# Projecting the FOX heads 0 to 3 with Strassen chunks that follow the z units

## The chip, the cores and the metric

The kernel runs on one core of a Trainium2 chip. TensorE (PE) multiplies matrices and writes into PSUM; ScalarE (ACT) and VectorE (DVE) work on tiles in SBUF and PSUM; GpSimd (POOL) works on SBUF alone, and it also issues the transfers that add to what they overwrite; SyncE (SP) issues the other transfers between device memory and SBUF. The metric is the time of one launch on the device in microseconds (us), lower is better.

## The reference

One hybrid decoder block over 512 tokens of width 1024, everything float32:

```python
u = rmsnorm(x, norm_mix_g[l])
proj = u @ w_in[l]
(gq, gk, gv, gz, ga, gb, fq, fk, fv, ff, gate_a, gate_b) = jnp.split(proj, split_idx, axis=-1)
...                                   # branch A: conv + SiLU on q, k, v; gated delta rule; norm * silu(z)
o_a = gated_delta_rule_chunked(qh, kh, vh, g, beta).transpose(0, 2, 1, 3)
...                                   # branch B ("FOX"): 8 heads of 128, normalised q and k
o_b = forgetting_attention(fqh, fkh, fvh, log_f).transpose(0, 2, 1, 3)
...
merged = jax.nn.sigmoid(gate_a) * y_a + jax.nn.sigmoid(gate_b) * y_b
h = x + merged @ w_out[l]
x = h + jnp.square(jax.nn.relu(rmsnorm(h, norm_mlp_g[l]) @ w_up[l])) @ w_down[l]
```

The change concerns one part of `proj`: the q, k and v columns of FOX heads 0 to 3, which are 1536 of its columns, `u` (512 x 1024) times a 1024 x 1536 piece of the weights.

## The kernel before

**Numbers.** Every large product is made from float32 operands split in two: `hi` is the operand rounded to the faster matmul type (an ACT cast) and `lo` is the remainder (a DVE subtraction). A product is three matmuls, hi·hi, lo·hi and hi·lo. Weights come as units of 128 x 1024; `seq` lists all units in their order, `unit()` takes the next one, keeps transfers `LA_RAW` = 3 units ahead and the splits `LA_SPLIT` = 2 units ahead.

**Two ways to project.** `dense` (lines 275, 276, 279) makes one block of 128 output columns as 24 matmuls that stream 512 tokens each. `fox_pair` (lines 962, 963, 965) makes the plain product of a panel of 256 columns of FOX heads, with tokens stationary and 256 columns of weights streamed. `stream` (line 1012) makes a chunk of 512 columns by Strassen's scheme (Winograd's form): the 512 x 1024 input and the 1024 x 512 weights are cut in four quarters each, and seven products P1 to P7 of quarters and of sums of quarters take the place of eight. The weights' sums are made by transfers: P1, P2, P3 and P5 are loaded by SP, and P5, P6, P4 and P7 arise when POOL issues a transfer that adds a quarter to the buffer of the product before it (P1, P5, P6, P4 share a buffer, and P3, P7 share one; P5's quarter is added to P1's). The input's sums are made once, by `factors_u`, in the dictionary `uforms`. A product is 24 matmuls of 256 columns. `to` takes the results out of PSUM: ACT copies the first product of a quarter of the output (line 992), DVE adds or subtracts a later one (line 994).

**Order of the work.** The main line is a straight sequence of products. Beside it, generators in `tasks` move on by one step at each `tick()`: the heads of the gated delta rule (`head`), the group's chain (`group_chain`: `invert`, which eliminates on DVE in lines 682 and 684 and multiplies in lines 708 to 742, and then `scan` over four chunks, lines 790 to 819), `decays`, `factors_u` and the `fox_worker`s, each of which takes one FOX head at a time from the list `fq`. A `dense` unit has two ticks, a Strassen product one. `hold[0]` keeps workers from taking a new head. The framework then plans the order on each engine, with the program's order as priority and its own estimate of times, so that what is ready may go ahead of what waits.

The main line before is:

1. The norm and the first z units (`zgate`), `NZ1` = 5 of them, with `normalise` making `uhi` and `ulo`, the split input, and storing the normalised input `xt` to device memory (`ud`).
2. `gdn_group(0)`: 12 projections (heads 0 to 3, three each).
3. `fox_pair(0)`, then `factors_u` is started (it loads `ud` back into tiles named `ux`), then `fox_pair(1)`. Meanwhile group 0's chain runs. One worker is there.
4. `zgate` 5 to 7, then `gdn_group(1)`, 12 projections, under `hold`. The decays of group 1 start when group 0's chain has ended.
5. `stream` over seven chunks: three for FOX heads 4 to 7, four for the two gates. Meanwhile group 1's chain runs, and two workers finish the FOX heads. Near its end `merge_gdn` needs every output of the gated delta rule, through `outputs_in`.
6. The merges, `w_out`, and the MLP, all Strassen products too (line 1172), until the end.

The matrix `AT`, which `head` fills (line 642) and `scan` reads (line 798), has one buffer (`atp`, `bufs=1`) for both groups. Most tiles of 128 x 512 come from one pool of `NPG` = 53 pages.

Of the kernel before, what the change touches and what calls it, by code (L numbers as in the profile page):

```python
# [19 lines left out]
H = 8  # L20
# [19 lines left out]
LA_SPLIT = 2  # L40
INV_STEP = (2500, 900)


def hybrid_block(tc, a, out):
# [65 lines left out]
    def cs(c):  # L110
        return slice(c * P, (c + 1) * P)
# [39 lines left out]
    seq = [("w_ab", 0)] + [("w_z", i) for i in range(NZ1)]  # L151
    seq += [("w_gdn", i) for i in range(12)] + [("w_fox", i) for i in range(12)]
    seq += [("w_z", i) for i in range(NZ1, H)] + [("w_gdn", 12 + i) for i in range(12)]

# [45 lines left out]
    def load(n):  # L200
        nme, i = seq[n]
        if nme in FACTOR:
            w, c, s_ = i
            q, old = FACTOR[nme]
            if old is None:
                if w == "w_st":
                    raw = (swp if nme == "P1" else wraw).tile([P, D], F32, tag="raw", name=nm("sraw"))
                else:
                    raw = fresh[2 if nme == "P2" else s_].tile([P, D], F32, tag="raw", name=nm("draw"))
                nc.sync.dma_start(raw, a[w][c, q, s_])  # L210
            elif (nme, i) in LONE:
                if n not in begun:
                    begin(n)
                raw = begun[n]
                nc.gpsimd.dma_start(raw, a[w][c, 2, s_], accum_op=ALU.add)
            else:
                raw = factors[old, i]
                assert seq.index((old, i)) < len(units)
                nc.gpsimd.dma_start(raw, a[w][c, q, s_], accum_op=ALU.add)
            factors[nme, i] = raw  # L220
            raws[n] = raw, [slice(0, D)]
            return
        w = 256 if nme == "w_ab" else D
        raw = wraw.tile([P, D], F32, tag="raw", name=nm("raw"))
        cuts = [slice(0, 512), slice(512, D)] if 0 < n < 3 else [slice(0, w)]
        for c in cuts:
            nc.sync.dma_start(raw[:, c], a[nme][i][:, c])
        raws[n] = raw, cuts
# [6 lines left out]
    def prefetch_new(n):  # L235

        for m in range(pos[0], min(len(seq), n)):
            if fresh and m not in raws and seq[m][0] in FACTOR and FACTOR[seq[m][0]][1] is None and seq[m][1][0] != "w_st":
                load(m)
            if seq[m] in LONE and m not in begun:  # L240
                begin(m)
# [168 lines left out]
    def normalise():  # L410
        for k in range(KT):
            pool.tensor_tensor(xt[k], xt[k], rb, op=ALU.mult)
            split(xt[k], mix_g[:, k:k + 1], dst=(uh(k), ul(k)))
            nc.sync.dma_start(ud[k], xt[k])
            if k % 2:
                yield


    ud = drp.tile([KT, P, T], F32, tag="ud", name="ud")
    uforms = {}  # L420
# [4 lines left out]
    def factors_u():  # L425
        lo, hi = slice(0, 256), slice(256, 512)
        for part in range(2):
            c = {}
            for k in (2 * part, 2 * part + 1, 2 * part + 4, 2 * part + 5):
                c[k] = page(s="ux")  # L430
                nc.sync.dma_start(c[k], ud[k])
            yield
            yield
# [226 lines left out]
    def invert(AT, rest, ahead):  # L660
# [34 lines left out]
        XT3 = v3(XT[:, :], NI)  # L695

        X2 = sbp.tile([P, NI, 64], F32, tag="sub", name=nm("X2"))
        pool.memset(X2[0:32, :, 32:64], 0.0)
# [140 lines left out]

    def gdn_group(g, box):  # L840
        AT = atp.tile([P, NI, P], F32, tag="AT", name=nm("AT"))
        hd = drp.tile([5, NCH, P, G, P], F32, tag=f"hd{g}", name=f"hd{g}")
        hts = []
        for i in range(G):
            h = g * G + i
            ys = []
            for j in range(3):
                ys.append(project(h, j))
                tick()
            hts.append(start(head(h, AT, *ys, box, hd)))  # L850
        return start(group_chain(g, AT, hd, hts))

# [97 lines left out]

    def fox_pair(hp):
        vts = ([], [])
        for pn in range(3):
            us = [unit("w_fox"), unit("w_fox")]
            pg2 = [page(s="fqk"), page(s="fqk")]
            for t2 in range(2):
                ps = mmps("fx")
                for tb in (2 * t2, 2 * t2 + 1):
                    o = ps[:, (tb % 2) * 256:(tb % 2 + 1) * 256]
                    for k in range(KT):  # L960
                        w = us[k // 4][0][:, (k % 4) * 256:(k % 4 + 1) * 256]
                        mm(o, uhi[k][:, cs(tb)], w, start=(k == 0), stop=False)  # L962
                        mm(o, ulo[k][:, cs(tb)], w, start=False, stop=False)  # L963
                    for k in range(KT):
                        mm(o, uhi[k][:, cs(tb)], us[k // 4][1][:, (k % 4) * 256:(k % 4 + 1) * 256], start=False,  # L965
                           stop=(k == KT - 1))
                    if tb % 2 == 0:
                        tick()
                if pn < 2:
                    act.copy(pg2[t2], ps)  # L970
                else:
                    for j in range(2):
                        (vec.tensor_copy if j else act.copy)(
                            v3(pg2[j][:, 2 * t2 * P:(2 * t2 + 2) * P], 2), v3(ps[:, :], 2)[:, :, cs(j)])
                tick()
            if pn < 2:
                fq.append((2 * hp + pn, pg2, vts[pn]))
            else:
                for v, x in zip(vts, pg2):
                    v += [x[:, cs(c)] for c in range(NCH)]  # L980

    def stream(parts, other):

# [11 lines left out]

        for p, c in STREAM:
            if p is None:
                other()
                continue
# [14 lines left out]
            done = parts[c][2]  # L1014
            at[0] = c
            if p == "P1":
# [73 lines left out]
    start(decays(0, box, gt))  # L1090
    fws = [start(fox_worker())]
    ch0 = gdn_group(0, box)
    fox_pair(0)
    fu = start(factors_u())
    fox_pair(1)
    start(decays(1, box, ch0))
    hold[0] = True
    for h in range(NZ1, H):
        zgate(h)
    ch1 = gdn_group(1, box)  # L1100
    hold[0] = False
    finish(fu)
    fws += [start(fox_worker()) for _ in range(1, NFW)]

# [37 lines left out]
    parts += [gate_chunk(i, to) for to in (sga, mg) for i in range(2)]  # L1142
    stream(parts, merge_gdn)

# [296 lines left out]
def _layout(inputs):  # L1441
# [20 lines left out]
    fx = w[:, 4112:7184].reshape(D, 3, H, P)  # L1462
    pan = []
    for hp in range(2):
        for h in (2 * hp, 2 * hp + 1):
            pan.append(np.concatenate([fx[:, 0, h], fx[:, 1, h]], axis=1))
        pan.append(np.concatenate([fx[:, 2, 2 * hp], fx[:, 2, 2 * hp + 1]], axis=1))
    o["w_fox"] = c(np.stack(pan).reshape(6, 2, 4, P, 256).transpose(0, 1, 3, 2, 4).reshape(12, P, D))
    q, k, v = [[fx[:, j, h] for h in range(H)] for j in range(3)]
# [3 lines left out]

    st = np.stack(st).reshape(7, 2, 4, P, 2, 256)
    o["w_st"] = c(np.stack([st[:, j, :, :, l] for j, l in ((0, 0), (0, 1), (1, 1), (1, 0))], 1)
                  .transpose(0, 1, 3, 2, 4).reshape(7, 4, 1, P, D))
    o["w_z"] = units(w[:, 3072:4096])
# [43 lines left out]
```

## Time and profile before

| what | before |
|---|---|
| median of 3 runs | 977.95 us (977.87 to 978.18) |
| the profiled execution, its own time | 979.09 us |
| its span, first to last instruction | 977.3 us |
| instructions | 17204 |
| PE busy | 968.0 us, 99% of the span |
| DVE, ACT, POOL busy | 709.4, 617.8, 219.5 us |
| granted TensorE clock | 1.000 |
| moved by DMA | 176.50 MB |

The profiled execution took 1.8 us more than its span, and 1.1 us more than the median run. A row of instruction groups gives line, engine, operation, output and inputs, shape and count, then the time that the group kept the engine busy, the mean duration of one in ns, and the idle time ahead of them. A row of the windows gives, for a stretch of the span, the busy time of PE, weight loads, DVE, ACT and POOL with the number of instructions, then the granted clock, the share of DMA and GB/s. A row of the chain gives start, length and what ran. Matmuls overlap, so the duration of one is longer than the spacing between two.

### The profile page before, as it was taken

What the parts mean: (1) busy time and instruction counts of PE and PEld (TensorE: products, weight loads), DVE (VectorE), ACT (ScalarE), POOL (GpSimd) and SP (SyncE); (2) the same over time, 40 slices, a digit from 0 to 9 for tenths busy, and PEclk for the clock granted to TensorE, in tenths of its full rate; (3) what the DMA queues carried; (4) which work ended last, traced back from release to release, by engine and by line L of the source; (5) the groups of instructions that cost most, each with busy time, mean ns of one, the idle gap of its engine ahead of it and who ended that gap; (6) DMA issues with size and microseconds to landing.
All of it is one profiled execution on the core that took longest, in us unless ns stands there. A gap on an engine that the chain in (4) does not pass through costs nothing.

```text
span 977.3 us, 17204 instructions
## 1 busy us (share of the span) xinstructions
PE 968.0 (99%) x6532; PEld 871.9 (89%) x6532; DVE 709.4 (73%) x1206; ACT 617.8 (63%) x1079; POOL 219.5 (22%) x220
## 2 busy tenths in 40 slices
PE   8999999999999999999999999999999999999998
PEld 6788899998888999999998888889989989988986
DVE  6877777656577799855656534889896697698596
ACT  7778654766764787868567412668755765666761
POOL 1503220202313423521320014412121121121110
PEclk9999999999999999999999999999999999999999
DMA  7646872475675987757888726678698888889883
GB/s 267 210 146 191 236 179 88 130 256 175 156 210 163 194 155 169 174 120 175 252 172 234 258 88 191 113 180 173 184 197 192 194 168 203 184 170 205 187 175 110
DMA packets 97634, 176.50 MB, mean 181 GB/s; under 512 B 8160, under 2 KB 53376, under 8 KB 97552
## 3 DMA queue, kind: packets, MB, share of 16 engines
q1 hardware_dynamic: 83088, 122.92, 40.6%
q0 software_dynamic: 14464, 52.49, 30.8%
q8 instruction: 51, 0.84, 0.4%
q14 instruction: 31, 0.25, 0.1%
HBM read 154.34 MB, written 21.04 MB: 179 GB/s over the span
## 4 chain that ended last, share of the span: by engine, by line
PE 91%; ACT 3%; DVE 2%; issue 2%; DMA 1%; POOL 0%; SPq 0%; ACTq 0%; POOLq 0%; DVEq 0%
PE mlp L1172 36%; PE st L1012 13%; PE mm L279 7%; PE mm L276 7%; PE mm L275 7%; PE fx L965 2%; PE fx L962 2%; PE fx L963 2%; PE fo L945 2%; PE sc L920 2%; PE pT L936 1%; ACT hi L256 1%; PE kq L648 1%; PE kk L640 1%; DMA row<-oad 1%
## 5 line engine op out<-in xcount | busy, mean ns | idle before, releaser
L1403 ACT CAST hi<-draw 128x1024 fp32r<-128x1024 f32 x124 | 130.1, 1050 | 118.4 <-PE mlp L1172 101.5
L1410 DVE TENSOR_TENSOR lo<-draw,hi 128x1024 fp32r<-128x1024 f32 x124 | 151.2, 1221 | 44.9 <-ACT hi L1403 42.1
L256 ACT CAST hi<-raw 128x1024 fp32r<-128x1024 f32 (+1 forms) x62 | 62.7, 1020 | 77.6 <-PE mm L276 48.6
L1172 PE MATMUL mlp<-hi,shi 128*128 128x512 f32 x280 | 109.5, 391 | 0.1
L1172 PE MATMUL mlp<-hi,slo 128*128 128x512 f32 x280 | 109.1, 390 | 0.0
L1172 PE MATMUL mlp<-lo,shi 128*128 128x512 f32 x280 | 109.0, 389 | 0.0
L257 DVE TENSOR_TENSOR lo<-raw,hi 128x1024 fp32r<-128x1024 f32 (+1 forms) x62 | 75.4, 1222 | 28.3 <-ACT hi L256 13.6
L1172 PE MATMUL mlp<-slo,hi 128*128 128x256 f32 x448 | 90.3, 283 | 0.0
L1172 PE MATMUL mlp<-shi,lo 128*128 128x256 f32 x448 | 90.3, 283 | 0.0
L1172 PE MATMUL mlp<-shi,hi 128*128 128x256 f32 x448 | 90.3, 283 | 0.0
L276 PE MATMUL mm<-ulo,hi 128*128 128x512 f32 x216 | 84.9, 394 | 1.2 <-DVE ulo L290 1.2
L275 PE MATMUL mm<-uhi,hi 128*128 128x512 f32 x216 | 85.2, 396 | 0.0
L257 DVE TENSOR_TENSOR lo<-sraw,hi 128x1024 fp32r<-128x1024 f32 x49 | 61.6, 1257 | 23.5 <-ACT hi L256 20.1
L1172 PEld LDWEIGHTS mlp<-shi,hi 128*128 128x128 f32 x448 | 70.6, 192 | 0.9
L256 ACT CAST hi<-sraw 128x1024 fp32r<-128x1024 f32 x49 | 51.3, 1047 | 30.7 <-PE st L1012 14.8
L1172 PEld LDWEIGHTS mlp<-shi,lo 128*128 128x128 f32 x448 | 69.9, 192 | 0.0
L1172 PEld LDWEIGHTS mlp<-slo,hi 128*128 128x128 f32 x448 | 69.8, 192 | 0.0
L1172 PEld LDWEIGHTS mlp<-hi,shi 128*128 128x128 f32 x280 | 52.6, 188 | 11.1 <-issue 0.7
L1172 PEld LDWEIGHTS mlp<-lo,shi 128*128 128x128 f32 x280 | 52.6, 188 | 11.1
L1172 PEld LDWEIGHTS mlp<-hi,slo 128*128 128x128 f32 x280 | 52.6, 188 | 10.3
L600 DVE SCALAR_TENSOR_TENSOR conv<-mm,c_conv,conv 128x511 f32<-128x511 f32 (+2 forms) x72 | 53.5, 744 | 5.6 <-ACT conv L597 4.4
L279 PE MATMUL mm<-uhi,lo 128*128 128x512 f32 x216 | 57.1, 402 | 0.0
(337 smaller groups left out, 2389.7 us busy)
## 6 DMA issues: line engine op xcount, KB each, us to landing
draw<-w_u POOLq DMA_DIRECT2D x32, 512.0 KB, 6.0
draw<-w_d POOLq DMA_DIRECT2D x32, 512.0 KB, 6.0
sraw<-w_st POOLq DMA_DIRECT2D x28, 512.0 KB, 6.0
draw<-w_d SPq DMA_DIRECT2D x26, 512.0 KB, 4.3
raw<-w_gdn SPq DMA_DIRECT2D x24, 512.0 KB, 4.3
draw<-w_u SPq DMA_DIRECT2D x24, 512.0 KB, 4.5
sraw<-w_st SPq DMA_DIRECT2D x21, 512.0 KB, 5.2
hd<-hd SPq DMA_DIRECT2D x34, 256.0 KB, 5.5
```

The lines of the kernel that those rows point to most:

```text
L256: act.copy(hi[:, c], raw[:, c])
L257: vec.tensor_tensor(lo[:, c], raw[:, c], hi[:, c].bitcast(F32), op=ALU.subtract)
L275: mm(o, w, rhi(k), start=(k == 0), stop=False)
L276: mm(o, w, rlo(k), start=False, stop=False)
L279: mm(o, lo[:, k * cols:(k + 1) * cols], rhi(k), start=False, stop=(k == KT - 1))
L600: vec.scalar_tensor_tensor(y[:, s:], ps[:, :T - s], cw[:, i:i + 1], y[:, s:], op0=ALU.mult, op1=ALU.add)
L920: mm(psc[:, :n], qT[:, s], kT[:, :n], start=True, stop=True)
L945: mm(po[:, cs(i)], vt[c], st[i][:, cs(c)], start=(c == 0), stop=(c == i))
L1012: mm(o, u, w, start=first and t == 0 and k == 0 and j == 0 and x is hi, stop=x is lo and k == 3, skip_group_check=True)
L1172: return (lambda *args, **kw: tc.keep_in_program_order(f(*args, **kw))) if self.pinned[0] else f
L1403: pact.copy(hi, raws[m][0])
L1410: pvec.tensor_tensor(lo, raws[m][0], hi[:, :].bitcast(F32), op=ALU.subtract)
```

## The change

FOX heads 0 to 3 are projected by `stream` instead of `fox_pair`, as three chunks laid out like those of heads 4 to 7 (new weights `w_sf`; `w_fox` and `fox_pair` go). The list `EARLY` orders their 21 products; near its end, two projections of group 1 and the start of group 1's decays are put between them. The z units 5 to 7 move ahead of the chunks, right behind group 0's projections. `factors_u` is started inside `gdn_group(0)`, after its second head, and works in place on the pages `xt`, which are no longer stored to and loaded from device memory. Both FOX workers exist from the start. Group 0's elimination takes smaller steps between ticks (`INV_STEP`), and `invert` has one more `yield`. Group 1's decays no longer wait for group 0's chain.

```diff
-INV_STEP = (2500, 900)
+INV_STEP = (900, 900)
...
-    seq += [("w_gdn", i) for i in range(12)] + [("w_fox", i) for i in range(12)]
-    seq += [("w_z", i) for i in range(NZ1, H)] + [("w_gdn", 12 + i) for i in range(12)]
+    seq += [("w_gdn", i) for i in range(12)]
+    EARLY = [("P1", 0), ("P2", 0), ("P5", 0), ("P1", 1), ("P3", 0), ("P6", 0), ("P2", 1), ("P7", 0), ("P5", 1), ("P4", 0),
+             ("P3", 1), ("P6", 1), ("P1", 2), ("P2", 2), ("P7", 1), ("P5", 2), ("P4", 1), ("P3", 2), ("P6", 2), (None, 0),
+             ("P7", 2), (None, 1), ("P4", 2), (None, "d")]
+    seq += [("w_z", i) for i in range(NZ1, H)]
+    seq += [(p, ("w_sf", c, 0)) if p else ("w_gdn", 12 + c) for p, c in EARLY if c != "d"]
+    seq += [("w_gdn", 14 + i) for i in range(10)]
...
             split(xt[k], mix_g[:, k:k + 1], dst=(uh(k), ul(k)))
-            nc.sync.dma_start(ud[k], xt[k])
...                                    # in factors_u
             for k in (2 * part, 2 * part + 1, 2 * part + 4, 2 * part + 5):
-                c[k] = page(s="ux")
-                nc.sync.dma_start(c[k], ud[k])
-            yield
+                c[k] = xt[k]
             yield
...                                    # in invert, behind the elimination
+        yield
         X2 = sbp.tile([P, NI, 64], F32, tag="sub", name=nm("X2"))
...
-    def gdn_group(g, box):
+    def gdn_group(g, box, between=None, ahead=()):
...
-                ys.append(project(h, j))
+                ys.append(ahead.pop(0) if ahead else project(h, j))
                 tick()
             hts.append(start(head(h, AT, *ys, box, hd)))
+            if between and i in between:
+                between[i]()
...
-    fws = [start(fox_worker())]
-    ch0 = gdn_group(0, box)
-    fox_pair(0)
-    fu = start(factors_u())
-    fox_pair(1)
-    start(decays(1, box, ch0))
-    hold[0] = True
+    fws = [start(fox_worker()) for _ in range(NFW)]
+    fu = []
+    ch0 = gdn_group(0, box, {1: lambda: fu.append(start(factors_u()))})
     for h in range(NZ1, H):
         zgate(h)
-    ch1 = gdn_group(1, box)
+    finish(*fu)
+    v01, v23 = ([], []), ([], [])
+    ahead = []
+    stream([fox_chunk((None, v01), (0, v01[0])), fox_chunk((2, v23[0]), (1, v01[1])), fox_chunk((3, v23[1]), (None, v23))],
+           EARLY, lambda c: start(decays(1, box)) if c == "d" else ahead.append(project(G, len(ahead))), False)
+    hold[0] = True
+    ch1 = gdn_group(1, box, ahead=ahead)
     hold[0] = False
-    finish(fu)
-    fws += [start(fox_worker()) for _ in range(1, NFW)]
```

More of the change, by code (lines that the diff above doesn't have):

```diff
@@ L205, in load @@
             if old is None:
-                if w == "w_st":
+                if w in ("w_st", "w_sf"):
                     raw = (swp if nme == "P1" else wraw).tile([P, D], F32, tag="raw", name=nm("sraw"))
@@ L237, in prefetch_new @@
         for m in range(pos[0], min(len(seq), n)):
-            if fresh and m not in raws and seq[m][0] in FACTOR and FACTOR[seq[m][0]][1] is None and seq[m][1][0] != "w_st":
+            if fresh and m not in raws and seq[m][0] in FACTOR and FACTOR[seq[m][0]][1] is None and seq[m][1][0] not in ("w_st", "w_sf"):
                 load(m)
@@ L413, in normalise @@
             split(xt[k], mix_g[:, k:k + 1], dst=(uh(k), ul(k)))
-            nc.sync.dma_start(ud[k], xt[k])
             if k % 2:
                 yield
-    ud = drp.tile([KT, P, T], F32, tag="ud", name="ud")
     uforms = {}
@@ L949, in fox_worker, with stream @@
             stores.append(start(store_late(obd[h], o)))
[L951 to L982, printed above, removed]
+    def stream(parts, order, other, main):
         bank = {}
@@ L994, in to @@
                     vec.tensor_tensor(x, x, ps, op=op)
-        for p, c in STREAM:
+        for p, c in order:
             if p is None:
-                other()
+                other(c)
                 continue
@@ L1014, in stream @@
             done = parts[c][2]
-            at[0] = c
+            if main:
+                at[0] = c
             if p == "P1":
@@ L1142, in hybrid_block @@
     parts += [gate_chunk(i, to) for to in (sga, mg) for i in range(2)]
-    stream(parts, merge_gdn)
+    stream(parts, STREAM, lambda c: merge_gdn(), True)
     ot2 = start(outputs_in2())
@@ L1462, in _layout @@
     fx = w[:, 4112:7184].reshape(D, 3, H, P)
[L1463 to L1468, printed above, removed]
     q, k, v = [[fx[:, j, h] for h in range(H)] for j in range(3)]
@@ L1472, in _layout @@
     st += [w[:, n + T * i:n + T * i + T] for n in (7192, 8216) for i in range(2)]
-    st = np.stack(st).reshape(7, 2, 4, P, 2, 256)
-    o["w_st"] = c(np.stack([st[:, j, :, :, l] for j, l in ((0, 0), (0, 1), (1, 1), (1, 0))], 1)
-                  .transpose(0, 1, 3, 2, 4).reshape(7, 4, 1, P, D))
+    sf = [np.concatenate(b, axis=1) for b in
+          ((v[0], v[1], q[0], k[0]), (q[2], k[2], q[1], k[1]), (q[3], k[3], v[2], v[3]))]
+    for name, m in (("w_sf", sf), ("w_st", st)):
+        m = np.stack(m).reshape(len(m), 2, 4, P, 2, 256)
+        o[name] = c(np.stack([m[:, j, :, :, l] for j, l in ((0, 0), (0, 1), (1, 1), (1, 0))], 1)
+                    .transpose(0, 1, 3, 2, 4).reshape(len(m), 4, 1, P, D))
     o["w_z"] = units(w[:, 3072:4096])
```

## The prediction

> **What bounds the kernel now.** I read the page's engine totals first, then the chain, then windows over the stages that the change touches.
>
> ```profile
> span 977.3 us, 17204 instructions
> PE 968.0 (99%) x6532; PEld 871.9 (89%) x6532; DVE 709.4 (73%) x1206; ACT 617.8 (63%) x1079; POOL 219.5 (22%) x220
> ```
>
> PE is busy for 968.0 of 977.3 us, so at most 9.3 us of visible idle time stand against any work taken off it. The windows say where that idle time is not:
>
> ```profile
> 90.00:120.00 30.00, 30.00 (x158) 25.33 (x157) 23.84 (x48) 20.14 (x49) 10.78 (x10) 1.00 0.88 221
> 120.00:137.00 17.00, 17.00 (x141) 16.80 (x140) 10.36 (x22) 9.88 (x29) 2.41 (x3) 1.00 0.78 206
> 137.00:218.00 81.00, 81.00 (x833) 78.46 (x833) 55.61 (x143) 47.14 (x86) 12.94 (x11) 1.00 0.50 156
> 218.00:242.00 24.00, 24.00 (x152) 21.00 (x151) 16.64 (x46) 15.98 (x27) 4.50 (x5) 1.00 0.61 188
> 242.00:320.00 78.00, 77.87 (x396) 65.27 (x395) 53.89 (x94) 47.59 (x110) 21.94 (x21) 1.00 0.64 173
> 320.00:400.00 80.00, 80.00 (x646) 77.28 (x645) 68.36 (x171) 61.19 (x132) 30.74 (x29) 1.00 0.82 176
> 515.00:532.00 17.00, 16.74 (x113) 15.04 (x112) 10.98 (x15) 11.35 (x22) 0.48 (x1) 1.00 0.87 244
> ```
>
> The second number after the length is PE. From 90 to 242 us, which holds the last half of group 0's projections, the plain FOX panels (120 to 218) and the three z units, PE never idles visibly. It also does not idle from 320 to 400, where the existing Strassen chunks of FOX heads 4 to 7 run beside group 1's heads and elimination, although DVE is at 68.36 of 80 us there. So the stage to be replaced is bound by matmul issue, and so is the stage that it will look like. Taking matmuls away should shorten the kernel by their spacing, unless the added work on the other engines makes PE wait.
>
> **What one matmul costs.** Durations overlap, so the price is the spacing, which the chain shows for unbroken runs (start, length, line, count):
>
> ```profile
> 79.32 1.83 PE mm L279 x8
> 123.16 0.96 PE fx L965 x8
> 321.51 2.87 PE st L1012 x24
> 494.14 8.63 PE st L1012 x72
> ```
>
> 0.96/8 = 0.120 us for the plain panels, and 2.87/24 = 0.1196 and 8.63/72 = 0.1199 us for Strassen products. The two kinds cost the same, 0.120 us. The 512-column matmuls of a z unit or a projection cost 1.83/8 = 0.229, so such a unit of 24 takes 5.5 us. The Trainium skill, TensorE: Matmul & The Clock Gate, section "Wait — 56ns, not 53.3ns?", gives N columns divided by 2.4 GHz plus 2.5 ns, 109 ns for 256 columns; the trace's 120 ns disagrees, the trace decides, and by the page the saving below would be 7.9 us.
>
> **The change, part by part.**
>
> *Matmuls removed.* The panels are these:
>
> ```profile
> L962 PE MATMUL fx<-hi,uhi 128*128 128x256 f32 x192 | 48.5, 288 | 0.0
> L963 PE MATMUL fx<-hi,ulo 128*128 128x256 f32 x192 | 47.8, 284 | 0.0
> L965 PE MATMUL fx<-lo,uhi 128*128 128x256 f32 x192 | 28.4, 285 | 0.0
> ```
>
> 3 x 192 = 576 matmuls. After: 3 chunks x 7 products x 24 = 504, of the same 256 columns. 72 fewer, x 0.120 = **8.64 us less** on PE, the path. Everything else on PE (z units, projections, attention, chains) is only moved.
>
> *Work added on ACT, DVE and POOL.* The existing chunks price it:
>
> ```profile
> L256 ACT CAST hi<-sraw 128x1024 fp32r<-128x1024 f32 x49 | 51.3, 1047 | 30.7 <-PE st L1012 14.8 <-DMA sraw<-w_st 7.8 <-PE mm L276 7.1
> L257 DVE TENSOR_TENSOR lo<-sraw,hi 128x1024 fp32r<-128x1024 f32 x49 | 61.6, 1257 | 23.5 <-ACT hi L256 20.1 <-PE mm L279 3.5
> L992 ACT COPY fqk<-st 128x512 f32<-128x512 f32 x12 | 7.0, 584 | 0.0
> L994 DVE TENSOR_TENSOR fqk<-fqk,st 128x512 f32<-128x512 f32 x9 | 6.1, 675 | 2.2 <-ACT fqk L992 2.0 <-ACT hi L256 0.2
> L257 DVE TENSOR_TENSOR lo<-raw,hi 128x1024 fp32r<-128x1024 f32 (+1 forms) x62 | 75.4, 1222 | 28.3 <-ACT hi L256 13.6
> L600 DVE SCALAR_TENSOR_TENSOR conv<-mm,c_conv,conv 128x511 f32<-128x511 f32 (+2 forms) x72 | 53.5, 744 | 5.6 <-ACT conv L597 4.4
> L970 ACT COPY fqk<-fx 128x512 f32<-128x512 f32 x8 | 4.7, 581 | 3.2 <-PE fx L965 3.2
> L973 ACT COPY fqk<-fx 128x256 f32<-128x256 f32 x4 | 1.5, 374 | 3.8 <-PE fx L965 3.8
> L973 DVE COPY fqk<-fx 128x256 f32<-128x256 f32 x4 | 1.7, 418 | 1.0 <-ACT fqk L973 1.0
> L219 POOL DMA_DIRECT2D sraw<-w_st x28 | 24.8, 886 | 91.6 <-DVE lo L257 56.8 <-DVE X L684 12.4 <-DVE fsm L932 9.2
> ```
>
> There are 21 units to split instead of 12: 9 x 1.047 = 9.4 us more on ACT, and 9 x 1.257 = 11.3 on DVE. The results leave PSUM in 12 ACT copies (7.0 us) and 9 DVE adds (6.1), in place of the panels' ACT copies (4.7 + 1.5) and DVE copies (1.7): +0.8 on ACT and +4.4 on DVE. POOL issues 9 accumulating transfers, 9 x 0.886 = 8.0 us, each behind the split of the product ahead. Cover: stream 1 gets about 75 us of PE time. For its DVE I take 55.6 us of the window 137 to 218, less the quarter sums that move out (13.6, below), less some ten of the old splits (10 x 1.22 = 12), plus 21 x 1.257 = 26.4 for the new ones, 6.1 for the adds, and 6.9 for the two projections (each a split and three conv steps of 0.744): 69.4 of some 80 us, 87%. The window 320 to 400 has 85% and no idle PE. I therefore price it near nothing; the worst rate that a chunk stage with waits shows is the window 515 to 532, 0.26 of 17 us (1.5%), which over 65 us is **+1.0 us**. Lower end 0; upper end under the second rival. Behind a waiting accumulate on POOL's queue stand the workers' and the scan's square roots and scalings, for which the chains wait, not the main line.
>
> *Quarter sums of the input, moved early.*
>
> ```profile
> L435 ACT ACTIVATE ux<-ux,c_norm_mix_g 128x512 f32<-128x512 f32 x8 | 5.3, 719 | 1.0 <-DMA ux<-ud 0.8
> L286 ACT CAST hi<-ux 128x512 fp32r<-128x512 f32 x8 | 4.9, 616 | 0.9 <-DVE ux L447 0.7
> L447 DVE TENSOR_TENSOR ux<-ux,ux 128x256 f32<-128x256 f32 x12 | 6.1, 551 | 0.1
> L447 DVE TENSOR_TENSOR ux<-ux 128x256 f32<-128x256 f32 x4 | 1.9, 523 | 0.0
> L287 DVE TENSOR_TENSOR lo<-ux,hi 128x512 fp32r<-128x512 f32 x8 | 5.6, 696 | 4.4 <-ACT hi L286 4.4
> ```
>
> ACT 10.2 us, DVE 13.6, unchanged in amount. They ran beside the panels and the z units and now run in the 11 ticks behind group 0's second head. A projection has two ticks, so that is about 30 us, the window 90 to 120: DVE 23.8 + 13.6 = 37.4 of 30 us, ACT 20.1 + 10.2 = 30.3 of 30. That overruns DVE by 7.4 us. It is covered for two reasons: splits are made two units ahead (two projections, 2 x 24 matmuls), and right behind come the three z units, which ask DVE for little more than their splits. The first sum is needed by P5, two products into the stream, so being late costs nothing before that. Price 0, up to 7.4 if the cover fails.
>
> *Transfers.*
>
> ```profile
> raw<-w_fox SPq DMA_DIRECT2D x12, 512.0 KB, 7.7
> ud<-x SPq DMA_DIRECT2D x8, 256.0 KB, 2.8
> ux<-ud SPq DMA_DIRECT2D x8, 256.0 KB, 5.3
> sraw<-w_st POOLq DMA_DIRECT2D x28, 512.0 KB, 6.0
> ```
>
> SP loses 16 issues of 256 KB (4.2 MB) and keeps 12 weight loads; POOL gains 9 of 512 KB (4.7 MB). In bytes it is even, and SP's queue gets shorter. A chain link in the weights (issue 0.9, landing 6.0, cast 1.05, split 1.26 = 9.2 us) is longer than two products (5.75), but the same order of products already runs at 321 us without idle PE. Price 0.
>
> *Smaller steps, z units, workers.* The z units are moved whole. The smaller elimination steps and the extra yield delay group 0's chain by ticks, not by engine time. With two workers, heads 0, 1 and 2 are taken before the hold, which leaves one old head to the late stream where the single worker left two: a relief there for which I take nothing.
>
> **Sum:** -8.64 + 1.0 = -7.6 us. Made on the profiled execution: 979.1 - 7.6 = 971.5; its span 977.3 becomes 969.7. The median run stood 1.1 below that execution, so the median becomes 977.95 - 7.6 = **970.3 us**.
>
> **Rivals.**
>
> *AT is still being read (slower).* Group 1's first write to AT must wait for the last `v` matmul of group 0's scan.
>
> ```profile
> 200.10 0.89 PE S L807 x8
> 240.83 0.89 PE v L798 x8
> 275.05 0.89 PE kk L640 x8
> ```
>
> From the first S to the last `v` the scan took 40.7 us; then 34 us passed before group 1's first `kk`. Counting ticks behind group 0's projections: six for the z units, in which the last head ends; the elimination then starts with the stream, needs some 12 ticks at the smaller step, and seven more follow before the scan. That is about the nineteenth product, where the first of the two early projections stands, and 16.7 us of main line (two projections at 5.5, two products at 2.9) are left before the stream's end; the last `v` then falls 24 us behind that end. Head 4 needs one more projection (5.5) and some four ticks (10) until it writes AT: 15.5 us. So its `kk` product may be 8 to 10 us early. If the planner lets the next projections pass, it costs nothing; if pages or PSUM banks stop them, PE waits up to 10: -8.6 + 1 + 10 = +2.4, **980.3 us**. It decides from a wait of 7.6 on. Against it: projections do not touch AT, and there are nine of them.
>
> *DVE or ACT becomes the bound.* The 7.4 us overrun reaches PE, or pages run short while xt is held longer. Between half and all of it is lost: 974 to **977.7 us**.
>
> *Accumulating loads come late.* Row: 6.0 us to land from POOL's queue. If each of the nine added loads made PE wait for one second DVE split, 9 x 1.26 = 11.3, less what two-unit lookahead hides, the gain is about gone: 977 us. The Trainium skill, SBUF — State Buffer, section "SBUF: two separate sides", warns that VectorE instructions that take the port shared with GpSimd starve such transfers of descriptors; no row here shows that: with DVE at 85% the existing ones land in 6.0 us.
>
> *More gain.* Pauses shorter than the 0.16 us by which durations (285 ns) exceed spacing do not show as idle. With one FOX head fewer in the late stream, and SP freed, some go: -8.6 and up to 2 more, **967.5 us**.
>
> **How the numbers follow.** About 0.2%, 2 us, is what a measurement of this kernel can tell from no change. Forecast (968.5 to 973) 0.60; more gain 0.12; DVE or ACT 0.12, half of it within 0.2%; late loads 0.04, mostly within; AT 0.12, mostly slower. Faster 0.78, same 0.11, slower 0.11. The range 967 to 978.5 leaves out the deepest gain and nearly all of the AT case.
>
> **What would show it.** Right: no fx groups, 1680 matmuls on line 1012, spacing still 0.120, PE at 99% with no idle window between 90 and 320 us, and span near 970. Wrong: idle PE ahead of group 1's `kk` or its projections (AT); idle PE on the splits or conv between 90 and 140 (DVE); ACT casts in the new stream waiting for `sraw` (loads). The prediction fails if PE idles over 6 us anew, or if the spacing of the new products is above 0.125 us.

## The result, and the profile after

The changed kernel is slower: 984.57 us median (982.80 to 986.59, four runs), against 978.07 us (977.87 to 978.98, four runs) for the kernel before on the same chip. The ratio is 1.0062, 95% interval 1.005 to 1.0075. The profiled execution is the slowest of its four runs; its span is 7.5 us longer than that of before.

The head of the page of the changed kernel, and its two busiest DMA queues (packets, MB, share of the 16 DMA engines' span):

```profile
span 984.8 us, 17110 instructions
PE 966.0 (98%) x6460; PEld 868.2 (88%) x6460; DVE 724.8 (74%) x1220; ACT 625.3 (63%) x1086; POOL 231.7 (24%) x232
...
q1 hardware_dynamic: 80352, 117.15, 37.9%
q0 software_dynamic: 16192, 58.78, 34.1%
```

The same two queues before:

```profile
q1 hardware_dynamic: 83088, 122.92, 40.6%
q0 software_dynamic: 14464, 52.49, 30.8%
```

The 72 matmuls are gone (6532 to 6460), yet PE is busy for only 2.0 us less, and the span less PE's busy time grew from 9.3 to 18.8 us. Five of the windows that the prediction showed of before, now of after (length, then busy time of PE, weight loads, DVE, ACT and POOL, the granted clock, DMA share and GB/s):

```profile
90.00:120.00 30.00, 28.12 (x142) 23.49 (x142) 26.93 (x49) 24.05 (x62) 12.04 (x9) 1.00 0.87 236
120.00:137.00 17.00, 17.00 (x91) 14.18 (x90) 15.70 (x31) 6.79 (x10) 2.25 (x2) 1.00 0.62 162
137.00:218.00 81.00, 75.57 (x713) 73.04 (x712) 61.41 (x135) 51.52 (x96) 23.65 (x23) 0.96 0.72 162
218.00:242.00 24.00, 24.00 (x190) 20.24 (x185) 12.70 (x32) 17.48 (x37) 3.68 (x3) 1.00 0.46 155
242.00:320.00 78.00, 75.45 (x454) 65.62 (x453) 49.79 (x111) 48.44 (x107) 22.44 (x20) 0.98 0.67 194
```

PE now lacks 1.88, 5.43 and 2.55 us in three of them, and the clock falls below 1 in two. The chain of waits has a name for each. PE's waits in 85 to 330 us (line waited for, us in total, times, longest):

```profile
PE st L986 <- ACT fqk L966: 5.4, 1, 5.4
PE ktm L119 <- ACT conv L604: 2.3, 1, 2.3
PE mm L281 <- ACT hi L262: 1.9, 1, 1.9
```

Three single waits, then, not a slow drift. I measured their whole price from the starts of all matmuls: of each spacing I took off the median spacing of its kind (line and shape) and summed what was left above 0.03 us. That gives 23.9 us of lost time before and 38.8 after: 14.9 us more, less 8.64 for the removed matmuls, is +6.3 of the 7.5 us by which the spans differ. Of the 14.9 us, 7.6 lie at 155 to 180 us, 1.9 at 90 to 130 and 4.1 at 296 to 312, the three places below.

**Place 1, 162 to 173 us.** PE's rows of after (start, length, operation, count; in brackets the idle time before and its releaser):

```profile
167.30 1.23 PE L986 MATMUL st<-hi,uhi 128*128 128x256 f32 x4 [5.43 <-ACT fqk L966]
...
171.74 1.05 PE L986 MATMUL st<-lo,uhi 128*128 128x256 f32 x4
172.59 0.84 PE L986 MATMUL st<-hi,hi 128*128 128x256 f32 x4
173.27 0.64 PE L986 MATMUL st<-hi,lo 128*128 128x256 f32 x4
```

The product waits for `fqk` on ACT, the copy that empties its PSUM bank. ACT's rows show why the copy is late:

```profile
164.28 1.04 ACT L262 CAST hi<-sraw 128x1024 fp32r<-128x1024 f32 x1 [9.91 <-DMA sraw<-w_sf]
165.23 0.58 ACT L966 COPY fqk<-st 128x512 f32<-128x512 f32 x1
165.71 1.05 ACT L262 CAST hi<-sraw 128x1024 fp32r<-128x1024 f32 x1
166.66 0.59 ACT L966 COPY fqk<-st 128x512 f32<-128x512 f32 x1
```

ACT takes its work in order. At its head stood the cast of P7's weights of chunk 0, and that waited 9.91 us for an accumulating load; two copies that needed no weights stood behind it. POOL issued that load at 151.41 us, the middle one of three close together:

```profile
148.27 0.87 POOL L225 DMA_DIRECT2D sraw<-w_sf  x1 [2.08 <-DVE lo L263]
151.41 0.87 POOL L225 DMA_DIRECT2D sraw<-w_sf  x1 [2.27 <-DVE tmp L684]
153.36 0.86 POOL L225 DMA_DIRECT2D sraw<-w_sf  x1 [1.08 <-DVE tmp L684]
```

Their median from issue to landing, in the DMA rows of 147 to 154 us, and the windows around them:

```profile
sraw<-w_sf POOLq DMA_DIRECT2D x3, 512.0 KB, 12.8
```

```profile
148.00:156.00 8.00, 8.00 (x69) 8.00 (x68) 7.86 (x12) 4.31 (x6) 3.25 (x4) 1.00 0.97 195
156.00:164.00 8.00, 5.87 (x49) 5.66 (x48) 1.98 (x8) 0.00 (x0) 0.00 (x0) 1.00 1.00 239
164.00:172.00 8.00, 4.70 (x22) 4.70 (x23) 6.47 (x14) 5.41 (x9) 0.88 (x1) 0.64 0.40 84
```

The DMA engines are full from 148 to 164 us: head 3's four stores, a row load and a z store had been issued from 143 to 149 us, just ahead of the weights. DVE stands still too (1.98 of 8 us), because its split of the same weights stands ahead of group 0's elimination. The third window adds a second loss: after 5.43 us without matmuls the clock is 0.64, and groups of four start 0.85 us apart until 172.59 (0.213 us a matmul instead of 0.120). Some 24 matmuls at 0.093 more are 2.2 us.

The Trainium skill, SBUF — State Buffer, section "SBUF: two separate sides", says that loads from GpSimd's queue can starve of descriptors while the DMA engines idle. The trace differs: here the engines are busy for 0.97 and 1.00 of the time. So idle engines are not what these loads wait for.

**Place 2, 115 us.** PE, then ACT:

```profile
116.86 0.47 PE L281 MATMUL mm<-uhi,hi 128*128 128x512 f32 x1 [1.88 <-ACT hi L262]
```

```profile
115.31 0.62 ACT L292 CAST hi<-ux 128x512 fp32r<-128x512 f32 x1 [0.57 <-DVE ux L449]
115.83 1.04 ACT L262 CAST hi<-raw 128x1024 fp32r<-128x1024 f32 x1
```

The cast of a quarter sum waits for DVE, and the weight cast that PE needs stands behind it on ACT.

**Place 3, 290 to 306 us.** PE, then ACT:

```profile
302.93 1.12 PE L119 MATMUL ktm<-ident,conv 128*128 128x128 f32 x4 [2.31 <-ACT conv L604]
```

```profile
294.14 0.69 ACT L599 ACTIVATE conv<-mm,c_conv 128x512 f32<-128x512 f32 x1 [5.58 <-DMA hd<-kn]
```

The page that `conv` was to be written to came free only when head 4's `kn` had been stored, and ACT fell behind; PE's idle time and the low clock behind it (0.59 in 302 to 306 us) cost some 4.4 us.

### The profile page after: what moved, and what is told of

It reads as the page before. It is cut to its first block, busy times and chain, and to the rows that moved or that the text cites. A ratio compares the mean times of both kernels' runs of the same rounds, so it can differ in the third digit from the quotient of the medians.

```text
span 984.8 us, 17110 instructions
## 1 busy us (share of the span) xinstructions
PE 966.0 (98%) x6460; PEld 868.2 (88%) x6460; DVE 724.8 (74%) x1220; ACT 625.3 (63%) x1086; POOL 231.7 (24%) x232
## 4 chain that ended last, share of the span: by engine, by line
PE 86%; DMA 4%; DVE 4%; ACT 2%; issue 2%; POOL 1%; SPq 0%; DVEq 0%; POOLq 0%; ACTq 0%
PE mlp L1147 35%; PE st L986 19%; PE mm L281 6%; PE mm L285 6%; PE mm L282 6%; DMA row<-rowd 2%; PE fo L950 2%; PE sc L925 2%; DMA sraw<-w_sf 1%; PE pT L941 1%; PE v L801 1%; DVE conv L602 1%; DMA zc<-zd 1%; PE o L822 1%; DVE lo L263 1%
## 5 line engine op out<-in xcount | busy, mean ns | idle before, releaser
L262 ACT CAST hi<-sraw 128x1024 fp32r<-128x1024 f32 x70 | 73.2, 1047 | 69.0 <-PE st L986 34.0
L263 DVE TENSOR_TENSOR lo<-sraw,hi 128x1024 fp32r<-128x1024 f32 x70 | 86.9, 1243 | 27.3 <-ACT hi L262 19.6
L262 ACT CAST hi<-raw 128x1024 fp32r<-128x1024 f32 (+1 forms) x50 | 50.3, 1012 | 57.2 <-PE mm L282 46.4
L263 DVE TENSOR_TENSOR lo<-raw,hi 128x1024 fp32r<-128x1024 f32 (+1 forms) x50 | 61.8, 1240 | 26.0 <-ACT hi L262 18.4
L1147 PEld LDWEIGHTS mlp<-hi,slo 128*128 128x128 f32 x280 | 52.6, 188 | 10.4
L225 POOL DMA_DIRECT2D draw<-w_d x30 | 26.3, 878 | 130.4 <-DVE lo L1385 119.8
```

The lines of the kernel that those rows point to most:

```text
L262: act.copy(hi[:, c], raw[:, c])
L263: vec.tensor_tensor(lo[:, c], raw[:, c], hi[:, c].bitcast(F32), op=ALU.subtract)
L1147: return (lambda *args, **kw: tc.keep_in_program_order(f(*args, **kw))) if self.pinned[0] else f
```

## The experiments

Each is timed against the kernel before on the same chip, which took 978.07 to 979.05 us there. The times are medians of 4 to 9 runs. The last columns are the idle time of PE in us, length less PE's busy time, in five windows of the one execution that was profiled.

| kernel | median us | ratio (95%) | 100-130 | 130-180 | 180-270 | 270-340 | 340-520 | sum |
|---|---|---|---|---|---|---|---|---|
| before | 978.07 | 1 | 0 | 0 | 0 | 0.1 | 0.2 | 0.3 |
| after | 984.57 | 1.0062 (1.005-1.0075) | 1.9 | 5.4 | 0 | 2.6 | 0 | 9.9 |
| e1_minus72 | 976.76 | 0.9976 (0.9966-0.9986) | 0 | 2.8 | 0.4 | 0.5 | 0.2 | 4.0 |
| e2_zstore | 982.21 | 1.0033 (1.002-1.0046) | 1.3 | 3.4 | 1.2 | 2.4 | 0 | 8.4 |
| e3_factors_late | 992.02 | 1.0133 (1.0116-1.0149) | 1.0 | 7.5 | 3.9 | 1.1 | 0.8 | 14.2 |
| e4_z_back | 1000.74 | 1.0221 (1.0207-1.0235) | 5.2 | 4.2 | 3.1 | 7.4 | 0.8 | 20.7 |
| e5_filler | 988.64 | 1.0098 (1.008-1.0115) | 1.4 | 4.8 | 2.2 | 3.0 | 1.9 | 13.3 |
| e6_steps | 994.34 | 1.0154 (1.0139-1.0169) | 2.5 | 4.1 | 12.5 | 0 | 0.4 | 19.5 |
| e7_npg51 | 989.87 | 1.0113 (1.0093-1.0133) | 1.6 | 2.3 | 1.2 | 8.0 | 1.1 | 14.2 |
| e8_one_worker | 983.93 | 1.0052 (1.004-1.0064) | 1.9 | 3.4 | 1.0 | 5.2 | 0 | 11.5 |
| e10_swap | 983.63 | 1.005 (1.0036-1.0063) | 1.2 | 3.6 | 0 | 5.5 | 0.1 | 10.4 |
| e11_decays | 988.26 | 1.0099 (1.0081-1.0116) | 1.9 | 3.4 | 0 | 5.8 | 0 | 11.0 |
| e12_all | 981.57 | 1.0037 (1.0022-1.0052) | 1.8 | 0.7 | 0.8 | 3.3 | 2.5 | 8.9 |
| e13_f2 | 989.25 | 1.0108 (1.0094-1.0121) | 1.2 | 1.3 | 2.9 | 5.7 | 0.4 | 11.4 |
| e14_pool | 983.68 | 1.0058 (1.0046-1.007) | 3.5 | 0.7 | 0.6 | 4.2 | 0 | 9.0 |
| e14y_yield | 988.08 | 1.0107 (1.0093-1.012) | 1.8 | 1.5 | 5.4 | 3.5 | 0.1 | 12.4 |
| e15_base | 984.53 | 1.0067 (1.0054-1.008) | 1.9 | 2.9 | 0 | 5.7 | 0 | 10.5 |
| e16_minus78 | 989.64 | 1.0112 (1.0099-1.0125) | 1.9 | 4.2 | 7.3 | 5.2 | 0 | 18.7 |

**What are the 72 matmuls worth by themselves?** In the kernel before, the last three of each panel's 24 accumulations are left out:

```diff
-                    for k in range(KT):
+                    for k in range(KT - 3):
                         mm(o, uhi[k][:, cs(tb)], us[k // 4][1][:, (k % 4) * 256:(k % 4 + 1) * 256], start=False,
-                           stop=(k == KT - 1))
+                           stop=(k == KT - 4))
```

> The kernel before, with the last 3 of the 24 matmuls of each token block of the FOX panels left out (72 of 576; the correction by the low part of the weights is then incomplete), so PE loses what the change takes off it and nothing else moves. If the stage is bound by matmul issue, as the prediction had it: 8.6 us less, 969.4 us. If something else set the pace there (transfers, DVE), clearly less than that: 973 to 978.

Measured: 976.76 against 979.05 us, 2.3 us less, not 8.6. PE's row and ACT's of this kernel:

```profile
175.50 0.26 PE L721 MATMUL Tp<-XT,Q 32*32 32x32 f32 x1 [2.45 <-ACT Q L711]
```

```profile
174.87 0.58 ACT L711 COPY Q<-Qp 32x512 f32<-32x512 f32 x1
```

ACT's row of the same copy before:

```profile
175.48 0.58 ACT L711 COPY Q<-Qp 32x512 f32<-32x512 f32 x1
```

ACT's copy comes only 0.6 us earlier, and DVE ends the elimination even later (its transposition `Xd` starts at 169.94 us, against 169.19 before). Before, PE took up `Tp` at 178.89 us, 2.8 us behind the end of that copy; with fewer matmuls ahead of it, PE gets there sooner and waits, and the clock falls (0.77 in 170 to 180 us). So "PE never idles" hid a second limit just behind PE. Of the 8.64 us, 6.3 do not come off even where nothing else is changed.

**Is place 1 the landing of one load?** Three edits of the changed kernel: z units 5 to 7 stored from ACT's queue, which takes SP's wait for them away (e2); another product put ahead of P7 (e10); both (e15).

```diff
-        nc.sync.dma_start(zd[h], z)
+        (nc.sync if h < NZ1 else act).dma_start(zd[h], z)
```

```diff
-  ("P2", 1), ("P7", 0), ("P5", 1), ("P4", 0),
+  ("P2", 1), ("P5", 1), ("P7", 0), ("P4", 0),
```

> The changed kernel with the stores of z units 5 to 7 issued from ACT's queue instead of SP's. Transfer theory: SP no longer stands 8 us behind a z store, head 3's stores leave earlier and not together with three accumulating loads; P7 of chunk 0 lands within 8 us instead of 12.7, the idle 5.4 us on PE at 162 shrinks below 1.5, the time falls by 5 to 8 us to 977 to 979.5. Rival (the early quarter sums and the late group 0 chain set the time): within 1.5 us of the changed kernel.

> The changed kernel with P5 of chunk 1 ahead of P7 of chunk 0 in the list EARLY. Transfer theory (the idle time of TensorE near 162 us is the landing time of P7's accumulating load less 7.19 us, since the weight cast behind it stands ahead of the evictions on ACT): the accumulating load now has one product more of time, about 3.1 us, so the idle time falls from 5.43 us to 1 to 3 us, the clock is not lowered at 164 to 172, and the time falls by 2 to 5 us, to 980 to 982.5. Rival, TensorE's path (the evictions are late whatever stands ahead of them): idle time of 5 us stays, 984 to 985.

> z units 5 to 7 stored from ACT's queue, and P5 of chunk 1 ahead of P7 of chunk 0; group 1's decays as in the changed kernel. If gains at the place near 162 us add: idle time there under 1 us and 979.5 to 981. If they move to a later place: 981.5 to 983, with idle time near 285 to 315 us in its stead, as in the swap alone.

e2 is 2.4 us below the changed kernel, between its two forecasts. PE's row and the load's, from issue to landing, first of e2, then of e8_one_worker (below):

```profile
161.62 0.74 PE L986 MATMUL st<-hi,uhi 128*128 128x256 f32 x4 [2.17 <-ACT fqk L966]
```

```profile
sraw<-w_sf POOLq DMA_DIRECT2D x1, 512.0 KB, 9.5
```

```profile
162.98 0.74 PE L986 MATMUL st<-hi,uhi 128*128 128x256 f32 x4 [2.53 <-ACT fqk L966]
```

```profile
sraw<-w_sf POOLq DMA_DIRECT2D x1, 512.0 KB, 9.9
```

In seven kernels that keep the order of the products and the place of the quarter sums, the landing time of P7's load less PE's idle time is the same: 12.77 - 5.43 (after), 11.54 - 4.20 (e16), 9.88 - 2.53 (e8), 9.52 - 2.17 (e2), 8.90 - 1.56 (e11), 8.76 - 1.41 (e7) and 8.40 - 1.07 (e6) are all 7.33 to 7.35 us. That is the slack of this place; each microsecond of landing time beyond it is one of idle PE. That shows what makes PE wait at place 1. (In e13, whose quarter sums start a head later, the difference is another one, 6.13 - 0.85 = 5.28.)

It does not show what makes the load late. Up to 174 us, e7, e8, e11 and e16 run the same instructions in the same order on every engine as the changed kernel (their edits show in that order only later), and yet the load took 8.76 to 11.54 us there and 12.77 in the profiled execution of the changed kernel. The 5.43 us are thus the most of what this place cost in five such executions, 1.41 to 5.43 us, and e2's 2.17 lie among them: that the z stores cause the late landing is not shown.

The swap alone did less than forecast (3.57 us of idle time, not 1 to 3): P5 of chunk 1 is an accumulating load too, so another late load came into the place, landing after 12.3 us. And e15, which joins both edits, gained nothing over the changed kernel, outside both forecasts, with 5.7 us idle at 270 to 340. Its row at place 1 is of use for the clock:

```profile
162.60 1.22 PE L986 MATMUL st<-hi,uhi 128*128 128x256 f32 x4 [2.89 <-ACT fqk L966]
```

After 2.89 us idle, four matmuls take 1.22 us, as after 5.43; after 2.53 they take 0.74. But the length of a wait does not settle it. The granted clock was 0.50 behind waits of 2.31 us at place 3 (302.8 to 306.1 us) and of 1.80 in e11 (172.8 to 176.1), and 1.00 behind 2.70 in e11 (335.0 to 338.4) and 3.45 in e14 (110.7 to 114.0). In the clock records of these traces, from 30 to 950 us, the half clock lasts 3.41 us, 6.83, or once 20.48: one, two or six times 3.41. The Trainium skill, TensorE: Matmul & The Clock Gate, section "What's actually happening", gives the gate a window of about 3.4 us that runs freely, whenever the work starts. The traces agree in the length, and a free-running window would explain why waits of like length end differently, which no run here tests.

**Were the parts priced at nothing free?** The quarter sums two heads later (e3), the z units back behind the chunks (e4), the two early projections moved into the middle of the stream (e5), the old elimination steps (e6):

```diff
-    ch0 = gdn_group(0, box, {1: lambda: fu.append(start(factors_u()))})
+    ch0 = gdn_group(0, box, {3: lambda: fu.append(start(factors_u()))})
```

> The changed kernel with the quarter sums started behind group 0's fourth head instead of its second, so that they run beside the z units. Quarter-sum theory: the 1.9 us of idle PE at 115 goes, and with DVE and ACT less loaded the splits run ahead again, so the time falls by 2 to 5 us. Transfer theory: only the 1.9 us go, and the stall in the stream stays or gets worse since the sums then fall nearer to P5: 982 to 986.

```diff
-    for h in range(NZ1, H):
-        zgate(h)
...
            EARLY, lambda c: ..., False)
+    for h in range(NZ1, H):
+        zgate(h)
```

> The changed kernel with z units 5 to 7 behind the chunks again, as before the change. Transfer theory: no z store stands on SP's queue at the start of the stream; the stall at 162 shrinks and the time falls by 4 to 8 us. Chain theory (group 0's chain starts too late behind z units and stream): the chain starts 16 us of PE time earlier against group 1's heads, AT is free in time, the stalls at 302 go too: 974 to 978. Quarter-sum theory: worse, since the sums have no z units to hide under: 985 to 990.

```diff
-  ("P3", 0), ("P6", 0), ("P2", 1), ("P7", 0), ... ("P6", 2), (None, 0), ("P7", 2), (None, 1), ("P4", 2),
+  ("P3", 0), ("P6", 0), (None, 0), ("P2", 1), ("P7", 0), ... ("P3", 1), (None, 1), ... ("P7", 2), ("P4", 2),
```

> The changed kernel with its two early projections of group 1 moved inside the stream: the first behind P6 of chunk 0, the second behind P3 of chunk 1, instead of near the end. They use no accumulated weights, so PE has 5.5 us of work while the three accumulating loads land late. Transfer theory: the stall at 162 (5.4 us idle and some 2 us at the low clock) goes or shrinks below 2 us, 4 to 8 us less than the changed kernel: 977 to 981. Rival (DVE and ACT are late in that stretch whatever the transfers do): the stall moves a few us and stays, 983 to 986.

```diff
-INV_STEP = (900, 900)
+INV_STEP = (2500, 900)
...
-        yield
```

> The changed kernel with the elimination steps of group 0 as before (INV_STEP 2500) and without the extra yield. Chain theory (group 0's chain ends too late; AT and pages are late for group 1, idle PE at 302): the elimination takes some 8 ticks less, the last v comes 10 to 20 us earlier, the idle time at 290 to 310 goes, 2 to 5 us less: 979.5 to 982.5. Rival: DVE, loaded with splits of Strassen products, is then blocked in longer pieces, the splits are late and PE waits in the stream: 985 to 990.

All four are slower than the changed kernel, by 7.4, 16.2, 4.1 and 9.8 us, and slower than any of their forecasts. One row of e4, one of e6, and the row of the changed kernel that answers to e6's:

```profile
133.24 1.19 PE L986 MATMUL st<-hi,uhi 128*128 128x256 f32 x4 [4.64 <-DVE conv L602]
```

```profile
190.06 1.92 PE L710 MATMUL Qp<-Xd,AT 32*32 32x32 f32 x64 [13.00 <-DVE Xd L692]
```

```profile
210.59 1.20 PE L711 MATMUL Qp<-Xd,AT 32*32 32x32 f32 x64
```

In e3 the wait of place 2 is gone, as in e13 below (0.95 and 1.21 us for another step of ACT stand at 106 us instead), but the cast of a quarter sum now stands ahead of a copy in the stream, and PE waits 5.92 us at 157. In e4 a product near the stream's start waits for DVE, whose steps that empty PSUM run there between quarter sums: the z units were the cover of the quarter sums, as the prediction had it. In e6 PE waits 13.00 us for the elimination, although that ends earlier than in the changed kernel: its last step starts at 188.7 us instead of 204.1 (169.0 before), and group 0's last `v` at 261.7 instead of 286.9. But in PE's order `Qp`, the first product behind the elimination, stands behind 264 of the stream's matmuls instead of 437, and PE meets it too soon. So the smaller steps and the extra yield move the products of the chain back on PE, to where they find the elimination done, and pay with a later chain. The chain theory had the earlier `v` right, and the idle time at 270 to 340 us does go; it did not have the wait. e5's added projections stood behind the same late cast (idle 3.71 us at 163 us) and did not fill the place.

**Place 3: pages, the worker, or the decays?** Two pages fewer (e7), one FOX worker until the late stream (e8), the decays behind group 0's chain again (e11):

```diff
-NPG = 53
+NPG = 51
```

> The changed kernel with 51 pages instead of 53 (there is no room for more than 53). Page theory for the idle PE at 302: with two pages fewer the waits for a page grow, the idle time between 230 and 320 rises by 3 us or more, 987 to 992. Rival (pages are not short, AT alone delays group 1): within 1.5 us of the changed kernel.

```diff
-    fws = [start(fox_worker()) for _ in range(NFW)]
+    fws = [start(fox_worker())]
...
+    fws += [start(fox_worker()) for _ in range(1, NFW)]
```

> The changed kernel with one FOX worker until the second stream, as before the change, so one old head more is left to that stream. Page theory: fewer pages are held while group 1 is projected, the idle time at 290 to 310 goes, 2 to 4 us less: 980.5 to 982.5. Rival: no effect there, and one more head in the late stream costs up to 2 us: 984.5 to 987.

```diff
-   EARLY, lambda c: start(decays(1, box)) if c == "d" else ..., False)
+   EARLY, lambda c: start(decays(1, box, ch0)) if c == "d" else ..., False)
```

> The changed kernel with group 1's decays waiting for group 0's chain to end, as in the kernel before, so their pages are not held during stream 1. Page theory of the idle time at 290 to 310 us: it falls from about 5 us to 2 to 3 us, the time to 981 to 983. Rival (group 1's chain is the late one there and needs its decays early): idle time there rises, 986 to 990.

e7's row on PE, and one on DVE ahead of it:

```profile
300.01 0.77 PE L281 MATMUL mm<-uhi,hi 128*128 128x512 f32 x1 [5.51 <-DVE sso L772]
```

```profile
295.45 0.75 DVE L780 SCALAR_TENSOR_TENSOR zc<-omT,c_gdn_norm_g,zc 128x512 f32<-128x512 f32 x1 [6.04 <-DMA zc<-zd]
```

Two pages fewer raise the idle time of 270 to 340 us from 2.6 to 8.0 and the time to what the page theory gave. But the rows show place 1's pattern on DVE: it waited 6.04 us for a load of z values (`zc`), with the `conv` steps that empty the projections' PSUM banks behind it. e10, e13 and e15 have the same wait with all 53 pages (DVE 4.30 to 4.46 us, PE 3.66 to 3.84), so e7 alone does not show that pages are short. And neither way of freeing some helped: with one worker the idle time there rose to 5.2 (and the time, 983.93 us, fell between the two forecasts), with late decays to 5.8 (waits of 3.05 us at 318.6 and 2.70 at 335.0). e11 as a whole is 3.7 us slower than the changed kernel, as its rival gave, though its profiled execution is 1.8 us shorter than that of the changed kernel, so no row shows where the 3.7 us arise. What makes place 3 late is not settled.

**Do the cures add up?** e12 takes e2, the swap and the late decays together; e13 is e2 with the quarter sums one head later; e14 is e15 with the quarter sums' casts on POOL, and e14y is e15 with those casts one step later:

```diff
-                xh_, xl_ = split(x)
+                xh_, xl_ = page(F32R, "hi")[:, :], page(F32R, "lo")[:, :]
+                pool.tensor_copy(xh_, x)
+                vec.tensor_tensor(xl_, x, xh_.bitcast(F32), op=ALU.subtract)
```

```diff
+                yield
                 xh_, xl_ = split(x)
```

> Three edits at once: z units 5 to 7 stored from ACT's queue (alone 982.2), P5 of chunk 1 ahead of P7 of chunk 0, and group 1's decays behind group 0's chain. If the three places are separate, their gains add: 2.4 us, about 1 us more near 162 us, and 2 us at 300 us: 978 to 980, level with the kernel before. If idle time that is taken out at one place comes back at group 0's next step, as in the kernel with 72 matmuls fewer, 981 to 984.

> z units 5 to 7 stored from ACT's queue, and the quarter sums started one head earlier than in e3, one head later than in the changed kernel. If only the place of the quarter sums among the weight casts matters at 115 us, the 2 us there go and the time is 980 to 981. If, as in e3, later quarter sums push work of DVE and ACT into the stream, idle time comes at 157 to 195 us in its place and the time is 984 to 989.

> As e15_base, with the eight casts of the quarter sums on POOL instead of ACT. If the place at 115 us is what it seems, the weight cast that stood behind them is on time, the idle time of 1.3 to 2 us there goes, and the time is 1.5 to 2 us below e15_base. If idle time moves on, it is the same as e15_base within 1 us. A cast on POOL that runs longer than on ACT delays the last quarter sums, and POOL's accumulating loads behind them: then idle time comes near 134 to 160 us.

> As e15_base, with each cast of a quarter sum one scheduling step behind its DVE operations, so that ACT does not stand in wait for DVE. The idle time at 115 us falls below 0.5 us and the time by 1 to 2 us against e15_base, if the eight more steps do not push the quarter sums past the start of the FOX products at 134 us; if they do, idle time of 2 us or more at 134 us and no gain.

They do not. In e12 place 1 shrinks to 0.65 us, the cure of the largest place, and 2.5 us appear in 340 to 520 instead, most of them in waits for FOX heads; it is 3.0 us better than the changed kernel, as the second forecast had it. e13 has no wait over 1 us in 130 to 180 either, but 2.63 us at 205 for the elimination and 3.78 at 301. e14 cures place 1 (no wait over 1 us in 130 to 180) but waits 3.45 us at 110.7 for DVE, which stood 3.26 us for a cast on POOL, and ends level with e15. e14y waits 5.4 us in 180 to 270 and gains nothing, without the idle time at 134 us that was forecast for that case. No version of the changed kernel came below the kernel before.

**Would more matmuls taken away help?** In the changed kernel, behind P7 of chunk 0, the last three of the four accumulations of the second weight half are left out of each product, 78 matmuls:

```diff
+        cut0 = pos[0]
...
-                    for k in range(4):
+                    for k in range(1 if x is lo and not main and pos[0] > cut0 + 8 else 4):
```

> The changed kernel without the last three of the four accumulations of the second weight half in the 13 FOX products behind P7 of chunk 0: 78 matmuls of 0.120 us, 9.4 us, left out of group 0's stream. If TensorE is what sets the time there, all of it comes off: 974 to 976. If the chains of groups 0 and 1 set it, as the kernel before with 72 fewer showed (2.3 of 8.6 us came off), 2 to 4 us come off, 980.5 to 982.5, and the idle time between 170 and 330 us grows by 5 to 7 us.

It is 5.1 us slower than the changed kernel, outside both forecasts. PE's wait for the elimination in it:

```profile
210.36 1.40 PE L711 MATMUL Qp<-Xd,AT 32*32 32x32 f32 x64 [2.57 <-DVE Xd L692]
```

And one window of the changed kernel, then of this one:

```profile
142.00:210.00 68.00, 62.57 (x482) 60.97 (x481) 55.13 (x128) 39.57 (x65) 19.44 (x22) 0.95 0.80 171
```

```profile
142.00:210.00 68.00, 57.48 (x421) 54.84 (x419) 56.30 (x124) 37.68 (x59) 19.75 (x20) 0.92 0.80 185
```

`Qp` starts at 210.59 us in the changed kernel and at 210.36 here, though PE runs 61 matmuls fewer in the window. DVE does as much in both, 55 to 56 of 68 us, and the elimination comes no earlier but later: `Xd` ends at 205.97 us in the changed kernel, 4.6 ahead of `Qp`, and at 210.22 here. The changed kernel has no idle time in 180 to 270 us and this one has 7.3: 2.57 for the elimination, 4.1 for ACT's steps of the FOX heads (`fk` 2.08, `pTs` 1.31 and 0.73). So 7.3 of the 9.4 us are given straight back, though only part of them to the chains of the two groups. The remaining loss, 2.7 us more idle time at 270 to 340 and the slow clock behind each wait, is measured but I have not traced its cause.

## Why the prediction was wrong

- *Spacing 0.120 us and 72 fewer.* Right: the products still start four in 0.48 us where the clock is 1.
- *8.64 us of them on the path.* This is the first step that failed. It rested on a PE without visible idle time from 90 to 242 us. e1 shows that such a PE can have another chain 2 to 3 us behind it, in the work of DVE and ACT for group 0, and only 2.3 us came off. Nor did the changed kernel gain from 78 matmuls fewer (e16).
- *Transfers at 0.* This is the costliest step: 5.43 us of idle time and 2.2 of slow clock in the profiled execution, 1.41 to 4.20 us of idle time in four others with the same instructions up to there. "In bytes it is even" was the wrong measure. An accumulating MB takes 30.8% x 977.3 / 52.49 = 5.73 us of all 16 engines, an MB of SP's queue 40.6% x 977.3 / 122.92 = 3.23. So the trade cost 11 us of DMA time (34.8 more and 23.6 less), and it fell into a stretch where the DMA share rose from 0.50 to 0.72 and head 3's stores also run. There are also 12 accumulating loads and 9 on SP, where I wrote 9 and 12: SP loads P1, P2 and P3 alone, and P5 accumulates. I took 6.0 us to land, a median over the whole kernel; these three had 12.8. The late stream that I leant on was no proof: its DMA share is 0.98 at its start and three loads there land in 9.0 us without idle PE, so its slack must be larger than the 7.34 us of this place. I gave late loads a chance of 0.04, with the mechanism of a wait for DVE; it was ACT's order, with two copies behind a cast, that turned a late load into idle PE.
- *Work added at +1.0.* The amounts were right (DVE +15.4 us against 15.7 forecast; ACT +7.5 against 10.2). The price cannot be told from the waits above: DVE is full in short stretches only (7.86 of 8 us at 148 to 156), but its order makes the elimination wait wherever a split waits for weights.
- *Quarter sums at 0.* 1.88 us, and e4 agrees with the cover by the z units. The overrun that was priced at up to 7.4 us came true in this small form.
- *Smaller steps at 0.* Wrong in kind: without them the kernel is 9.8 us slower (e6). They also delay the chain by much more than a few ticks: the last `v` of group 0 stands at 286.9 us, 46 behind its 240.8 of before, and 25 of these go when the old steps come back (261.7 in e6). I had it 24 us behind the stream's end; it stands 39 behind it (247.6).
- *The AT rival* gave 980.3, nearest to the result, but not for its reason: the first `kk` starts at 288.4, right behind the last `v`, and PE is not idle there, since projections fill the gap. Its next idle time, from 300.6 us on, is the one that begins with a page.

Two of the signs named for a failure were there to be read: ACT casts in the new stream waiting for `sraw` (9.91 us), and more than 6 us of new idle time on PE (9.9).

## What to carry to other kernels

A PE that is busy for 99% is no proof that the path is PE alone: take out some of the matmuls, leaving the rest as it is, and see how much comes off before counting on the whole. Price a moved transfer by the DMA engines' share in its new window and by the slack of its consumer there, and look at what else stands behind the consumer in its engine's order, above all copies that free PSUM banks. Where several chains are just in time, curing one wait mostly moves it: in the variants of the changed kernel the idle time summed to 8.4 us at least, about what the change saves. And look for a wait in a second execution before calling it the price of a change: the largest one here varied from 1.41 to 5.43 us with the same instructions ahead of it.

## What the hardware showed that I had not expected

- The clock was halved in stretches of 3.41 us or a multiple of it, behind waits as short as 1.80 us (e11) and not behind one of 3.45 (e14). The length of a wait alone did not foretell it.
- An accumulating load took 1.8 times the DMA engine time of SP's transfers for each MB, and 12.8 us to land (median of three) where the medians of such loads on the page are 5.5 to 6.7.
- Among DVE's short elimination steps, two were held up in the changed kernel: its 31 `X<-X,tmp` took 11.4 us in 142 to 210 us, against 7.9 before in 134 to 174, and the difference lies in two steps that took 1.24 us at 153.7 and 2.87 at 181.2 instead of 0.2 to 0.3. Each ended within 0.2 us of POOL instructions that ran beside it (`nd<-row` to 154.87, `fqk<-fqk,fss` to 183.90). That one holds up the other is likely, but no run tests it.
